# Two-part products one column part at a time, and 512-column products on normalised operands in the dense layers with 512 tokens

## The chip, the cores and the metric

The kernel runs on one core of one Trainium2 chip. The metric is device time in microseconds for one execution; lower is better. A second number, the span, runs from the first to the last instruction of one profiled execution.

## What is computed

The reference is a network of four layers over 512 latent tokens and 256 context tokens, with 1024 channels. Each layer is a token mixer (layers 0 and 3 Fourier, layer 1 differential attention, layer 2 latent attention) followed by a dense layer. Context tokens are updated in layers 0, 1 and 2 by the reference, but layer 3's mixer is the Fourier one, which reads no context in the last layer; so the kernel carries 768 tokens through the dense layers of layers 0 and 1 and 512 through those of layers 2 and 3.

```python
def rms_norm(x, g, eps=RMS_EPS):
    y = x32 * lax.rsqrt(jnp.mean(x32 * x32, axis=-1, keepdims=True) + eps)
    return y.astype(x.dtype) * g
def modulate(x, g, shift, scale):
    return rms_norm(x, g) * (1 + scale) + shift
def sq_relu_mlp(h, w1, w2):
    return jnp.square(jax.nn.relu(h @ w1)) @ w2
...
        x_lat = x_lat + g_m * sq_relu_mlp(modulate(x_lat, norm_mlp_g[i], sh_m, sc_m), mlp_w1[i], mlp_w2[i])
```

`w1` is 1024 x 4096 and `w2` is 4096 x 1024, all in float32.

## The kernel before

Channels lie on the 128 partitions and tokens on the free axis: `x[k]`, k = 0..7, holds 128 channels of all tokens. TensorE multiplies operands of a shortened float32 form, so each operand is split in two tiles, a high part and a low remainder (`split`: ScalarE casts the high part, VectorE subtracts), and every product of 128 rows takes three matmuls: high weight by high operand, high weight by low operand, low weight by high operand. `mm3g` issues them; its loops run over k, then over the three, then over the column parts, because one matmul takes at most 512 columns. Each matmul loads its 128 x 128 weights anew: the page counts as many weight loads (PEld) as matmuls (PE).

The dense layer is `mlp`. `MlpNorm.feed` makes its operand `h[k]` (tiles `hhi`, `hlo`, 776 columns): x times gain and scale, not yet divided by the token's norm, and behind the T tokens two columns with the shift vector. `w1(m)`, m = 0..31, multiplies eight `h[k]` into one PSUM tile `pw` of 1024 columns (three such buffers). With 768 tokens its two parts are 512 and 258 columns, with 512 tokens 256 and 258; 24 such pairs make a tile. VectorE copies the two shift columns to `bt` (L420) and multiplies the rest by the tokens' inverse norm `r_all` (L427); ScalarE adds `bt` in a Relu (L431), squares (L432) and casts `ahi`; VectorE forms `alo`. `w2(j)`, j = 0..7, takes four such tiles and multiplies them into eight output groups; `accum` (L371, VectorE) adds gate times result to `x[n]`. With 768 tokens a group is 12 pairs of 512 and 256 columns, with 512 tokens 12 matmuls of 512. The last, `w2(7)`, has code of its own that goes by chunks of 256 tokens.

The order on TensorE is written by hand, as the program is: w1(0) to w1(3), then for each j w1(4j+4), w2(j), w1(4j+5) to w1(4j+7). The other engines are ordered by the framework's scheduler by priority and dependence; `accum` has a raised one. VectorE also computes the next layer's modulation vectors in the dense layers (units of L264, called from `bg`). Weights come by DMA into ring buffers, five high and low pairs.

`lin_part`, which multiplies the Fourier mixer's result by its weights, has the same loops as `mm3g`, with parts of 512 and 256 columns in layer 0.

Of the kernel before, what the change touches and what calls it, by code (L numbers as in the profile page):

```python
# [19 lines left out]
KT = 8  # L20
# [24 lines left out]
def body(ctx: ExitStack, tc, a, out):  # L45
# [65 lines left out]
    def gload(srcs, n=512):  # L111
        """operands in the space that all phases share, for the start of the next phase among others"""
        w = []
        for src in srcs:
            raw = rawt()
            nc.sync.dma_start(raw[:, :n], src)
            hi, lo = (gp.tile([128, 512], F32R, name="g", tag="g", bufs=4) for _ in range(2))
            split(hi[:, :n], lo[:, :n], raw[:, :n])
            w.append((hi, lo))
        return w  # L120
# [26 lines left out]
    def mm3g(o, n, wfn, afn, parts, off=0):  # L147
        for k in range(n):
            (wh, wl), (ah, al) = wfn(k), afn(k)
            for i, (w, v) in enumerate(((wh, ah), (wh, al), (wl, ah))):  # L150
                for c0, w_ in parts:
                    mm(o[:, c0 - off:c0 - off + w_], w, v[:, c0:c0 + w_],
                       k == 0 and i == 0, k == n - 1 and i == 2)
                    yield cost(w_)
# [5 lines left out]
    def mm3(*args, **kw):  # L160
        run(mm3g(*args, **kw))

    class Fill:
        """Tensor-engine work put between the steps of an attention chain. What a generator gives
        first comes after its loads; the loads of the next one are issued when one starts."""
# [10 lines left out]
        def front(self, name, gens):  # L176
            """Ahead of what is held back."""
            i = [q[0] for q in self.q].index(self.held)
            self.q[i:i] = [[name, g, False] for g in gens]
            self.held = None  # L180
            if i < 2:
                self.prime(i)
# [111 lines left out]
    class MixNorm:  # L294
        """x -> h = x * rstd * g * (1 + scale) + shift, split, by chunks of 256 tokens."""
# [36 lines left out]
    class MlpNorm:  # L332
        """h' = x * g * (1 + scale), split, with the shifts in two columns after the tokens; the
        rstd of a token multiplies what a product with h' gives, the shift's product is added."""
# [39 lines left out]
    def out_gemm_g(K, wfn, afn, T, l, ch, norm=None):  # L374
        """x += gate * (W^T a)"""
        wide = state["psum"]["w"][0] >= T
        for n in range(KT):
            for g in ([parts(T)] if wide else [[q] for q in parts(T)]):
                p = pt_("w")
                o = g[0][0]  # L380
                yield from mm3g(p, K, lambda k: wfn(k, n), afn, g, off=o)
                for c0, w in g:
                    accum(n, c0, w, p[:, c0 - o:c0 - o + w], l, ch)
            if norm:
                norm.feed(n)
# [8 lines left out]
    def mlp(l, nm, nn):  # L394
# [4 lines left out]
        with ExitStack() as es:  # L399
# [10 lines left out]
            hparts, po = ([(0, 512), (512, 258)], 0) if T > SL else ([(0, 256), (256, 258)], 256)  # L410
            nbg = [0.0]

            def w1(m):
                w = wload(wp, a["w1"][l, m]) if m else pre.pop("w1")
                p = pt_("w")
                mm3(p, KT, lambda k: (kview if m else hview)(w, k), lambda k: h[k], hparts, off=-po)
# [4 lines left out]
                r = rp.tile([128, T], F32, name="r", tag="r", bufs=2)  # L421
                hi = ap_.tile([128, T], F32R, name="ahi", tag="a")
                lo = ap_.tile([128, T], F32R, name="alo", tag="a")
# [10 lines left out]
                nbg[0] += 1.6  # L434
                bg(int(nbg[0]))
                nbg[0] -= int(nbg[0])
                return hi, lo

            def w2(j, act):
                w = [wload(wp, a["w2"][l, j * CH + i]) for i in range(CH)]  # L440
                wfn = lambda k, n: kview(w[k], n)
                if j < NJ - 1:
                    run(out_gemm_g(CH, wfn, lambda k: act[k], T, l, G_M))
                    return
# [65 lines left out]
    def lin_part(p, w, Y, k0, k1, T):  # L510
        for k in range(k0, k1):
            (wh, wl), (yh, yl) = (hview if type(w) is list else kview)(w, k), Y[k]
            for i, (u, v) in enumerate(((wh, yh), (wh, yl), (wl, yh))):
                for c0, w_ in parts(T):
                    mm(p[:, c0:c0 + w_], u, v[:, c0:c0 + w_], k == 0 and i == 0, k == KT - 1 and i == 2)

    def fold(sp, p, ny, T, ys):
        """two tiles (d' = 0..127 and 256 - d', 128 first) of the product's real part"""
# [40 lines left out]
    def fourier_first(nm):  # L559
        l, T = 0, TT  # L560
        with ExitStack() as es:
# [66 lines left out]
            def mod_pe(ch, w):  # L628
                """a channel's vectors from weights with the inner dimension on partitions"""
# [136 lines left out]
    def transpose_g(p, dst_h, dst_l, q0, k0, n, tag="t"):  # L766
        """dst[:, kt, q0:q0+128] = transposes of the n blocks of p from k0, split."""
# [8 lines left out]
    def diff(l, h, nm):  # L776
        T = TT
        with ExitStack() as es:
# [85 lines left out]
            def gens(i, hd):  # L864
                """k (or q) of the latent tokens, then of the context."""
# [29 lines left out]
            def S(hd, c0, qi, cqi=None):  # L895
                """Weights of 128 latent queries, and with cqi of 128 context queries."""
# [88 lines left out]
            def last(hd, e):  # L985
                """The end of the latent queries of a head."""
# [457 lines left out]
```

## Time and profile before

| what | value |
|---|---|
| median of three runs | 2974.22 us (2969.59 to 2979.68) |
| span of the profiled execution | 2962.0 us |
| median less span | 12.2 us |
| TensorE matmul (PE) busy | 2843.3 us, 96% |
| VectorE (DVE) busy | 1947.8 us, 66% |
| ScalarE (ACT) busy | 1310.6 us, 44% |

The profiled execution has no time of its own on record beside its span; the 12.2 us between the span and the median of the runs lie outside what the profile shows. Matmuls overlap, so PE's busy time is the time in which at least one is under way; how fast they follow one another is read from the starts of matmuls.

### The profile page before, as it was taken

What the parts mean: (1) busy time and instruction counts of PE and PEld (TensorE: products, weight loads), DVE (VectorE), ACT (ScalarE), POOL (GpSimd) and SP (SyncE); (2) the same over time, 40 slices, a digit from 0 to 9 for tenths busy, and PEclk for the clock granted to TensorE, in tenths of its full rate; (3) what the DMA queues carried; (4) which work ended last, traced back from release to release, by engine and by line L of the source; (5) the groups of instructions that cost most, each with busy time, mean ns of one, the idle gap of its engine ahead of it and who ended that gap; (6) DMA issues with size and microseconds to landing.
All of it is one profiled execution on the core that took longest, in us unless ns stands there. A gap on an engine that the chain in (4) does not pass through costs nothing.

```text
span 2962.0 us, 42506 instructions
## 1 busy us (share of the span) xinstructions
PE 2843.3 (96%) x16875; PEld 2459.3 (83%) x16875; DVE 1947.8 (66%) x3468; ACT 1310.6 (44%) x2405; POOL 157.6 (5%) x167
## 2 busy tenths in 40 slices
PE   8999999999999999799999998899899999999998
PEld 5788888888777777688888887788799998799997
DVE  7986656568677767785445448888776665654454
ACT  4542223235565546533233336777643344543342
POOL 0100000002010000100000002000100001100001
PEclk9999999999999999899999999999999999999999
DMA  8453333331111111053333310000175551232231
GB/s 322 148 178 122 108 106 108 126 102 56 48 35 44 39 35 45 30 176 118 123 107 121 107 50 31 22 22 22 57 235 171 165 170 61 72 116 98 79 107 50
DMA packets 93542, 291.30 MB, mean 98 GB/s; under 512 B 10624, under 2 KB 14880, under 8 KB 92832
## 3 DMA queue, kind: packets, MB, share of 16 engines
q1 hardware_dynamic: 90784, 285.44, 28.8%
q0 software_dynamic: 2560, 3.15, 0.5%
q8 instruction: 133, 2.18, 0.3%
q14 instruction: 65, 0.53, 0.1%
HBM read 283.29 MB, written 2.11 MB: 96 GB/s over the span
## 4 chain that ended last, share of the span: by engine, by line
PE 83%; DVE 10%; ACT 4%; issue 1%; DMA 1%; POOL 1%; POOLq 0%; SPq 0%; ACTq 0%; DVEq 0%
PE pw L140 71%; PE ps L140 5%; PE pu L140 5%; PE pu L770 1%; DVE x L371 1%; DVE ptl L97 1%; ACT e L1251 1%; DVE hlo L330 1%; DVE nu L328 1%; DVE mx L1248 1%; ACT pth L96 1%; PE pn L140 0%; DVE wlo L97 0%; POOL nacc L357 0%; DVE qs L846 0%
## 5 line engine op out<-in xcount | busy, mean ns | idle before, releaser
L96 ACT CAST whi<-raw 128x1024 fp32r<-128x1024 f32 (+1 forms) x322 | 311.8, 984 | 1051.8 <-PE pw L140 1010.0
L371 DVE SCALAR_TENSOR_TENSOR x<-pw,mod,x 128x512 f32<-128x512 f32 (+1 forms) x504 | 302.3, 623 | 331.7 <-PE pw L140 330.5
L140 PE MATMUL pw<-hhi,whi 128*128 128x512 f32 (+1 forms) x2112 | 502.8, 315 | 5.1 <-ACT whi L96 3.5
L140 PE MATMUL pw<-hlo,whi 128*128 128x512 f32 (+1 forms) x2112 | 502.4, 314 | 0.0
L140 PE MATMUL pw<-hhi,wlo 128*128 128x512 f32 (+1 forms) x2112 | 502.4, 314 | 0.0
L140 PE MATMUL pw<-ahi,wlo 128*128 128x512 f32 (+1 forms) x1664 | 500.0, 344 | 0.0
L140 PE MATMUL pw<-ahi,whi 128*128 128x512 f32 (+1 forms) x1664 | 496.5, 342 | 0.0
L140 PE MATMUL pw<-alo,whi 128*128 128x512 f32 (+1 forms) x1664 | 494.9, 341 | 0.0
L97 DVE TENSOR_TENSOR wlo<-raw,whi 128x1024 fp32r<-128x1024 f32 (+1 forms) x322 | 361.6, 1140 | 45.8 <-ACT whi L96 42.0
L140 PEld LDWEIGHTS pw<-hhi,whi 128*128 128x128 f32 x2112 | 334.3, 190 | 32.1 <-ACT whi L96 3.9
L140 PEld LDWEIGHTS pw<-hhi,wlo 128*128 128x128 f32 x2112 | 332.9, 190 | 24.1 <-DVE wlo L97 0.3
L140 PEld LDWEIGHTS pw<-hlo,whi 128*128 128x128 f32 x2112 | 333.2, 191 | 23.7
L140 PEld LDWEIGHTS pw<-ahi,whi 128*128 128x128 f32 x1664 | 284.1, 189 | 40.7
L140 PEld LDWEIGHTS pw<-ahi,wlo 128*128 128x128 f32 x1664 | 282.7, 189 | 36.6
L140 PEld LDWEIGHTS pw<-alo,whi 128*128 128x128 f32 x1664 | 281.1, 188 | 38.0
L264 DVE SCALAR_TENSOR_TENSOR raw<-raw,cb 128x1024 f32<-128x1024 f32 x176 | 215.9, 1227 | 84.8 <-DMA raw<-in_modw 82.8
L97 DVE TENSOR_TENSOR alo<-r,ahi 128x768 fp32r<-128x768 f32 (+2 forms) x134 | 105.8, 792 | 84.1 <-ACT ahi L96 83.9
L431 ACT ACTIVATE r<-r,bt 128x512 f32<-128x512 f32 (+1 forms) x196 | 119.1, 640 | 73.5 <-DVE r L427 73.4
L420 DVE COPY bt<-pw 128x2 f32<-128x2 f32 x128 | 20.1, 157 | 196.4 <-PE pw L140 196.3
L264 DVE SCALAR_TENSOR_TENSOR junk<-raw,cb 128x1024 bf16<-128x1024 f32 x96 | 117.1, 1220 | 46.0 <-DMA raw<-in_modw 43.4
L307 POOL TENSOR_TENSOR nacc<-nacc,nsq 128x256 f32<-128x256 f32 x70 | 53.1, 758 | 1767.1 <-ACT nsq L306 1766.6
L97 DVE TENSOR_TENSOR ptl<-pu,pth 128x384 fp32r<-128x384 f32 (+1 forms) x208 | 107.0, 541 | 53.8 <-ACT pth L96 52.0
(321 smaller groups left out, 4336.4 us busy)
## 6 DMA issues: line engine op xcount, KB each, us to landing
raw<-in_w SPq DMA_DIRECT2D x252, 512.0 KB, 3.6
raw<-in_modw SPq DMA_DIRECT2D x176, 512.0 KB, 3.4
wm<-in_msh SPq DMA_DIRECT2D x32, 256.0 KB, 5.9
raw<-in_fw SPq DMA_DIRECT2D x10, 512.0 KB, 4.7
cb<-scr SPq DMA_DIRECT2D x4, 1024.0 KB, 5.4
raw<-in_dwk SPq DMA_DIRECT2D x16, 256.0 KB, 2.7
raw<-in_dwq SPq DMA_DIRECT2D x16, 256.0 KB, 2.8
raw<-in_dwv SPq DMA_DIRECT2D x16, 256.0 KB, 2.7
```

What stands on the lines that cost most here:

```text
L96: nc.scalar.copy(hi, src)
L97: nc.vector.tensor_sub(lo, src, rd(hi))
L140: r = nc.tensor.matmul(o, lhsT, rhs, start=start, stop=stop)
L264: nc.vector.scalar_tensor_tensor(o, m, 1.0, cb[:, v * 1024:(v + 1) * 1024], op0=ALU.mult, op1=ALU.mult, accum_out=mcol(mod[l, ch], v, k))
L307: nc.gpsimd.tensor_tensor(nacc[:, c0:c0 + w], nacc[:, c0:c0 + w], s, op=ALU.add)
L328: nc.vector.scalar_tensor_tensor(u, xs, am, r, op0=ALU.mult, op1=ALU.mult)
L330: nc.vector.scalar_tensor_tensor(lo, u, sh, rd(hi), op0=ALU.add, op1=ALU.subtract)
L371: nc.vector.scalar_tensor_tensor(xs, src, mcol(mod[l, ch], 0 if c0 < SL else 1, n), xs, op0=ALU.mult, op1=ALU.add)
L431: nc.scalar.activation(r[:, c0:c1], r[:, c0:c1], AF.Relu, bias=bt[:, v:v + 1])
L770: nc.tensor.transpose(t[:, i * 128:(i + 1) * 128], p[:, (k0 + i) * 128:(k0 + i + 1) * 128], ident)
L1248: nc.vector.reduce_max(mx, s[:, :T], axis=AX.X)
L1251: nc.scalar.activation(et, s[:, :T], AF.Exp, bias=mx, scale=MLA_SCALE)
```

## The change

`mm3g` and `lin_part` get the column part as outermost loop, so that all matmuls of the first part come ahead of those of the second. In dense layers with 512 tokens, `normed(k)` replaces `h[k]` in place during `w2(0)` by the fully normalised and shifted operand (it reads `x[k]` before `accum` of the same k writes it), and tiles m >= 5 then run as 24 single matmuls of 512 columns, with a Relu straight from PSUM and neither the copy to `bt` nor the multiplication by `r_all`. `tick` is the old end of `w1` under a name. Comments are removed.

```diff
     def mm3g(o, n, wfn, afn, parts, off=0):
-        for k in range(n):
-            (wh, wl), (ah, al) = wfn(k), afn(k)
-            for i, (w, v) in enumerate(((wh, ah), (wh, al), (wl, ah))):
-                for c0, w_ in parts:
+        for c0, w_ in parts:
+            for k in range(n):
+                (wh, wl), (ah, al) = wfn(k), afn(k)
+                for i, (w, v) in enumerate(((wh, ah), (wh, al), (wl, ah))):
                     mm(o[:, c0 - off:c0 - off + w_], w, v[:, c0:c0 + w_],
                        k == 0 and i == 0, k == n - 1 and i == 2)
                     yield cost(w_)
...
-    def out_gemm_g(K, wfn, afn, T, l, ch, norm=None):
-        """x += gate * (W^T a)"""
+    def out_gemm_g(K, wfn, afn, T, l, ch, norm=None, before=None):
...
         for n in range(KT):
+            if before:
+                before(n)
...
+            wide = T == SL
+            late = CH + 1 if wide else FF
...
+                if m >= late:
+                    mm3(p, KT, lambda k: kview(w, k), lambda k: h[k], [(0, T)])
+                    step = 256 if m == CH * NJ - 1 else T
+                    for o in range(0, T, step):
+                        s = slice(o, o + step)
+                        nc.scalar.activation(r[:, s], p[:, s], AF.Relu)
+                        nc.scalar.activation(r[:, s], r[:, s], AF.Square)
+                        split(hi[:, s], lo[:, s], r[:, s])
+                    tick()
+                    return hi, lo
...
+            def normed(k):
+
+                u = rp.tile([128, T], F32, name="cu", tag="cu", bufs=2)
+                hi, lo = (q[:, 0:T] for q in h[k])
+                sh = mcol(mod[l, SH_M], 0, k)
+                nc.vector.scalar_tensor_tensor(
+                    u, x[k][:, 0:T], mcol(amul[l, SC_M], 0, k), r_all, op0=ALU.mult, op1=ALU.mult)
+                nc.scalar.activation(hi, u, AF.Identity, bias=sh)
+                nc.vector.scalar_tensor_tensor(lo, u, sh, rd(hi), op0=ALU.add, op1=ALU.subtract)
...
-                    run(out_gemm_g(CH, wfn, lambda k: act[k], T, l, G_M))
+                    run(out_gemm_g(CH, wfn, lambda k: act[k], T, l, G_M, before=normed if wide and j == 0 else None))
...
     def lin_part(p, w, Y, k0, k1, T):
-        for k in range(k0, k1):
-            (wh, wl), (yh, yl) = (hview if type(w) is list else kview)(w, k), Y[k]
-            for i, (u, v) in enumerate(((wh, yh), (wh, yl), (wl, yh))):
-                for c0, w_ in parts(T):
+        for c0, w_ in parts(T):
+            for k in range(k0, k1):
+                (wh, wl), (yh, yl) = (hview if type(w) is list else kview)(w, k), Y[k]
+                for i, (u, v) in enumerate(((wh, yh), (wh, yl), (wl, yh))):
                     mm(p[:, c0:c0 + w_], u, v[:, c0:c0 + w_], k == 0 and i == 0, k == KT - 1 and i == 2)
```

On TensorE, at the start of the first output group of w2(0) in layer 0 (names: PSUM tile, then moving operand and weights), the order was, before:

```order
L140 MATMUL pw<-ahi,whi 128x512
L140 MATMUL pw<-ahi,whi 128x256
L140 MATMUL pw<-alo,whi 128x512
L140 MATMUL pw<-alo,whi 128x256
L140 MATMUL pw<-ahi,wlo 128x512
L140 MATMUL pw<-ahi,wlo 128x256
```

In the changed program the same group has twelve of 512 columns and then twelve of 256; the rows at the seam are:

```order
L140 MATMUL pw<-ahi,whi 128x512
L140 MATMUL pw<-alo,whi 128x512
L140 MATMUL pw<-ahi,wlo 128x512
L140 MATMUL pw<-ahi,whi 128x256
L140 MATMUL pw<-alo,whi 128x256
L140 MATMUL pw<-ahi,wlo 128x256
```

The number of matmuls is the same; a matmul now follows one of its own width everywhere but at the seam.

On TensorE in layer 2, where w2(0) ends and w1(5) begins, before:

```order
L140 MATMUL pw<-alo,whi 128x512
L140 MATMUL pw<-ahi,wlo 128x512
L140 MATMUL pw<-hhi,whi 128x256
L140 MATMUL pw<-hhi,whi 128x258
L140 MATMUL pw<-hlo,whi 128x256
L140 MATMUL pw<-hlo,whi 128x258
L140 MATMUL pw<-hhi,wlo 128x256
L140 MATMUL pw<-hhi,wlo 128x258
```

and in the changed program:

```order
L140 MATMUL pw<-alo,whi 128x512
L140 MATMUL pw<-ahi,wlo 128x512
L140 MATMUL pw<-hhi,whi 128x512
L140 MATMUL pw<-hlo,whi 128x512
L140 MATMUL pw<-hhi,wlo 128x512
```

Two matmuls of half the width became one; the operands `hhi` and `hlo` are now those that `normed` writes while w2(0) runs.

On VectorE in layer 2, over w2(0) (x_70 to x_77 are the eight tiles `x[k]`, L371 is `accum`, L264 a unit of the modulation), before:

```order
L371 SCALAR_TENSOR_TENSOR x_70<-pw,mod_5_116,x_70 128x512
L264 SCALAR_TENSOR_TENSOR raw,mod_0_117<-raw,cb 128x1024
L97 TENSOR_TENSOR alo<-r,ahi 128x512
L371 SCALAR_TENSOR_TENSOR x_71<-pw,mod_5_116,x_71 128x512
L264 SCALAR_TENSOR_TENSOR raw,mod_0_117<-raw,cb 128x1024 x2
L371 SCALAR_TENSOR_TENSOR x_72<-pw,mod_5_116,x_72 128x512
L371 SCALAR_TENSOR_TENSOR x_73<-pw,mod_5_116,x_73 128x512
```

and in the changed program, from the last piece ahead of x_74 on:

```order
L371 SCALAR_TENSOR_TENSOR x_74<-pw,mod_5_116,x_74 128x512
L464 SCALAR_TENSOR_TENSOR hlo<-cu,mod_3_113,hhi 128x512
L461 SCALAR_TENSOR_TENSOR cu<-x_77,am_4_115,rall 128x512
L371 SCALAR_TENSOR_TENSOR x_75<-pw,mod_5_116,x_75 128x512
L264 SCALAR_TENSOR_TENSOR raw,mod_0_117<-raw,cb 128x1024
L464 SCALAR_TENSOR_TENSOR hlo<-cu,mod_3_113,hhi 128x512
L371 SCALAR_TENSOR_TENSOR x_76<-pw,mod_5_116,x_76 128x512
```

Two pieces for each k (L461, L464) stand between the additions, those of the last k behind the addition to x_75; most units of the modulation have moved behind them.

## Rows read from the trace of the kernel before

**Rows 1.** The page: busy time, TensorE's granted clock in 40 slices, the chain

```profile
PE 2843.3 (96%) x16875; PEld 2459.3 (83%) x16875; DVE 1947.8 (66%) x3468; ACT 1310.6 (44%) x2405; POOL 157.6 (5%) x167
...
PEclk9999999999999999899999999999999999999999
...
PE 83%; DVE 10%; ACT 4%; issue 1%; DMA 1%; POOL 1%; POOLq 0%; SPq 0%; ACTq 0%; DVEq 0%
```

**Rows 2.** Windows: dense layers 0, 2; length, busy PE PEld DVE ACT POOL, clock, DMA

```profile
177.69:694.87 517.18, 517.18 (x2966) 452.78 (x2965) 330.23 (x516) 161.91 (x212) 5.34 (x8) 1.00 0.35 117
2147.99:2495.30 347.31, 347.31 (x2289) 320.89 (x2290) 220.18 (x334) 130.71 (x176) 5.42 (x8) 0.99 0.50 166
```

**Rows 3.** Timeline of PE, layer 0: first matmuls of w1(5), w2(1), w1(9)

```profile
247.33 0.51 PE L140 MATMUL pw<-hhi,whi 128*128 128x512 f32 x2
...
281.12 0.51 PE L140 MATMUL pw<-ahi,whi 128*128 128x512 f32 x2
...
315.04 0.40 PE L140 MATMUL pw<-hhi,whi 128*128 128x512 f32 x1
```

**Rows 4.** Timeline of PE, layer 2: first matmuls of w1(5), w2(1), w1(9)

```profile
2193.93 0.40 PE L140 MATMUL pw<-hhi,whi 128*128 128x256 f32 x2
...
2216.83 0.40 PE L140 MATMUL pw<-ahi,whi 128*128 128x512 f32 x1
...
2238.62 0.40 PE L140 MATMUL pw<-hhi,whi 128*128 128x256 f32 x2
```

**Rows 5.** Windows: w2(0) of layer 2, w2(0) of layer 3, then layer 3's next four tiles

```profile
2172.14:2193.93 21.79, 21.79 (x99) 18.02 (x97) 15.37 (x24) 5.00 (x7) 0.00 (x0) 1.00 0.61 208
...
2617.03:2638.82 21.79, 21.79 (x99) 18.03 (x97) 8.81 (x12) 5.04 (x7) 0.00 (x0) 1.00 0.07 25
2638.82:2661.78 22.96, 22.96 (x193) 22.96 (x192) 12.34 (x17) 10.90 (x15) 0.00 (x0) 1.00 0.48 161
```

**Rows 6.** Timeline of PE, layer 2's mixer: 512-column run with h, first and last

```profile
1812.52 0.40 PE L140 MATMUL ps<-hlo,whi 128*128 128x512 f32 x1
...
1823.17 0.39 PE L140 MATMUL ps<-hhi,wlo 128*128 128x512 f32 x1
```

**Rows 7.** Timeline of PE, layer 1's mixer: 256-column run with h, first and last

```profile
745.51 0.28 PE L140 MATMUL pw<-hhi,wlo 128*128 128x256 f32 x1
...
749.41 0.28 PE L140 MATMUL pw<-hhi,wlo 128*128 128x256 f32 x1
```

**Rows 8.** Timeline of PE, layer 0's w2(7): 256-column run with activations, first and last

```profile
685.75 0.28 PE L140 MATMUL pw<-ahi,wlo 128*128 128x256 f32 x1
...
691.51 0.28 PE L140 MATMUL pw<-ahi,wlo 128*128 128x256 f32 x1
```

**Rows 9.** Timeline of PE, layer 0's Fourier product by its weights

```profile
95.31 0.52 PE L140 MATMUL pw<-yh,whi 128*128 128x512 f32 x2
...
97.08 0.40 PE L140 MATMUL pw<-yh,wlo 128*128 128x512 f32 x1
```

**Rows 10.** Groups of VectorE and ScalarE by shape: busy us, mean ns, idle before

```profile
L264 DVE SCALAR_TENSOR_TENSOR raw<-raw,cb 128x1024 f32<-128x1024 f32 x176 | 215.9, 1227 | 84.8 <-DMA raw<-in_modw 82.8
L427 DVE TENSOR_TENSOR r<-pw,rall 128x512 f32<-128x512 f32 x62 | 42.1, 681 | 0.0
L348 DVE SCALAR_TENSOR_TENSOR hlo<-x,am,hhi 128x512 fp32r<-128x512 f32 x32 | 23.5, 744 | 2.5 <-ACT hhi L347 2.2
L347 ACT ACTIVATE hhi<-x,am 128x512 fp32r<-128x512 f32 x32 | 23.1, 723 | 43.0 <-DVE x L371 36.1 <-DVE am L254 6.8
```

**Rows 11.** Waits of PE around the start of dense layer 2 (us, times, longest)

```profile
PE pw L140 <- ACT whi L96: 3.5, 1, 3.5
PE pn L140 <- POOL nacc L357: 0.4, 1, 0.4
```

**Rows 12.** Windows: 5.73 us behind PE's wait at the start of dense layer 0

```profile
176.47:182.20 5.73, 5.73 (x17) 4.88 (x18) 5.73 (x13) 2.36 (x4) 0.00 (x0) 0.50 0.73 246
```

More of the change, by code (lines that the diff above doesn't have):

```diff
@@ L409, in mlp, with tick @@
                 bg_add(l + 1, (SC_A, SH_A, G_A, SC_M, SH_M, G_M))
-            hparts, po = ([(0, 512), (512, 258)], 0) if T > SL else ([(0, 256), (256, 258)], 256)
+            wide = T == SL
+            late = CH + 1 if wide else FF
+            hparts, po = ([(0, 256), (256, 258)], 256) if wide else ([(0, 512), (512, 258)], 0)
             nbg = [0.0]
+            def tick():
+                nbg[0] += 1.6
+                bg(int(nbg[0]))
+                nbg[0] -= int(nbg[0])
             def w1(m):
@@ L415, in w1 @@
                 p = pt_("w")
+                r = rp.tile([128, T], F32, name="r", tag="r", bufs=2)
+                hi = ap_.tile([128, T], F32R, name="ahi", tag="a")
+                lo = ap_.tile([128, T], F32R, name="alo", tag="a")
+                if m >= late:
[8 more added lines that the diff above has]
+                    return hi, lo
                 mm3(p, KT, lambda k: (kview if m else hview)(w, k), lambda k: h[k], hparts, off=-po)
@@ L420, in w1 @@
                 nc.vector.tensor_copy(bt, p[:, po + T:po + T + 2])
-                r = rp.tile([128, T], F32, name="r", tag="r", bufs=2)
-                hi = ap_.tile([128, T], F32R, name="ahi", tag="a")
-                lo = ap_.tile([128, T], F32R, name="alo", tag="a")
                 step = 256 if m == CH * NJ - 1 else T
@@ L433, in w1 @@
                     split(hi[:, s], lo[:, s], r[:, s])
-                nbg[0] += 1.6
-                bg(int(nbg[0]))
-                nbg[0] -= int(nbg[0])
+                tick()
                 return hi, lo
+            def normed(k):
[6 more added lines that the diff above has]
+                nc.vector.scalar_tensor_tensor(lo, u, sh, rd(hi), op0=ALU.add, op1=ALU.subtract)
             def w2(j, act):
```

## Prediction

> **What bounds the kernel now.** I read the page first: TensorE is busy 96% of the span, its granted clock is at nine tenths or more in 39 of 40 slices, and the chain that ended last lies on it for 83% [rows 1]. So the time is mostly the number of matmuls times their spacing. Next I cut out the dense layers by windows. In layers 0 and 2, between the start of w1(1) and the end of the whole-group part, PE is busy for the whole length (517.18 of 517.18 us, 347.31 of 347.31) at a clock of 1.00 and 0.99 [rows 2], which is the upper of the two levels, 2.4 GHz. VectorE is busy 64% and 63% of these windows and ScalarE 31% and 38% (330.23 and 161.91 of 517.18, 220.18 and 130.71 of 347.31). There is no gap to fill: here a change is worth what it does to the spacing of matmuls, less any wait that it creates. Third I took the spacing from the timeline, from the first matmul of a block of known size to the first of the next, since PE's busy time counts overlapping matmuls only as "under way".
>
> **The spacings.** A block between two such starts is four tiles of 24 pairs, or eight groups of 12: 96 in each.
> - Layer 0, pairs 512 and 258 (w1): (281.12 - 247.33)/96 = 352.0 ns. Pairs 512 and 256 (w2): (315.04 - 281.12)/96 = 353.3 ns [rows 3].
> - Layers 2 and 3, pairs 256 and 258 (w1): 22.90/96 = 238.5 ns [rows 4] and 22.96/96 = 239.2 ns [rows 5]; mean 238.9.
> - Layer 2, 512 alone with activations (w2): 21.79/96 = 227.0 ns [rows 4].
> - 512 alone with h: from the first to the last row 46 steps in 10.65 us, 231.5 ns [rows 6].
> - 256 alone with h: 33 steps in 3.90 us, 118.2 ns [rows 7]; 258 scaled by columns 119.1.
> - 256 alone with activations: 48 steps in 5.76 us, 120.0 ns [rows 8].
>
> So a pair of different widths costs more than its two halves cost in runs of one width. That is what the sum rests on.
>
> **The change part by part.**
> *A. w2 with 768 tokens.* 2 layers x 7 x 8 groups x 12 = 1344 pairs. Apart, 227.0 + 120.0 = 347.0 ns; together 353.3; so 6.3 ns a pair is to be had. One seam a group stays, so 11 of 12: 1344 x 6.3 x 11/12 = 7.8 us.
> *B. w1 with 768 tokens.* 2 x 32 x 24 = 1536 pairs. Apart, with h, 231.5 + 119.1 = 350.6; together 352.0; 1.4 ns each: 2.2 us. The bounds come from which row the 512 resembles. With h moving, as [rows 6], it is 231.5; at the 227.0 of [rows 4] the gain would be 5.9 ns, 9.1 us. I take the row with the same moving operand.
> *C. w1 with 512 tokens from the sixth tile.* 2 x 27 x 24 = 1296 pairs become single matmuls: 238.9 - 231.5 = 7.4 ns, 9.6 us; 15.4 us if they ran at 227.0.
> *D. The first five tiles there* keep two parts: 2 x 5 x 24 = 240 pairs at 238.9 - (118.2 + 119.1) = 1.6 ns: 0.4 us.
> *E. The Fourier product of layer 0*, 8 x 24 = 192 pairs: five steps in 1.77 us are 354.0 ns [rows 9]. Between nothing and 7.0 ns (the activations' 347.0): 0 to 1.3 us, I take 0.5.
> *F. The first tile of each dense layer.* With the part outermost, w1(0) wants all eight h[k] within its first half, not spread over the tile. In layers 0 and 1 the first part is 24 x 0.23 = 5.5 us of the 8.4. In layer 2 PE waits 3.5 us for weights and 0.4 for the norm at the start [rows 11], so most of a later w1(0) would only shorten the next wait. Below: nothing. Above: 4 us, about the two waits together once more. I take 1.0 us lost. The 5.73 us at a clock of 0.50 (the level of 1.2 GHz) that stand behind PE's wait for the norm in layer 0 [rows 12] are there in both versions, as that wait is for the statistics, not for h.
>
> *What the normalising costs.* `normed` adds, per k, a VectorE piece into `cu`, a ScalarE piece and a second VectorE piece. Nearest rows: 744 ns (L348) and 723 ns (L347) [rows 10]. Eight of each are 8 x 2 x 0.744 = 11.9 us of VectorE and 5.8 us of ScalarE, inside w2(0), which lasts 21.79 us. VectorE has 15.37 us of work there in layer 2 and 8.81 in layer 3 [rows 5]; with 11.9 more, 27.3 and 20.7 us. In layer 3 it fits. In layer 2 it is 5.5 us too much, but the units of the modulation (1.23 us each, L264 [rows 10]) are wanted only by the next layer, and in the changed order most stand behind the normalising. The last piece of k = 7 stands behind the addition to x_75, the sixth group, which ends 6 x 2.72 = 16.3 us into w2(0); three or four VectorE pieces later, about 20 us in, `h[7]` is there. w1(5) begins at 21.8 and needs k = 7 after 21 matmuls, at 26.6. So some 6 us of slack cover it, and I cost it at nothing; without that cover it is the slower rival below. What queues behind these pieces on VectorE is the addition that frees a PSUM buffer of w2(0); with three buffers and 2.72 us a group it may be two groups late, 5.4 us, and one or two pieces of 0.744 delay it by at most 1.5.
>
> *What goes.* 54 tiles lose the multiplication (681 ns [rows 10]) and the small copy on VectorE. That is not on the path. The Relu reads PSUM itself, so the way from the last matmul to `ahi` becomes shorter. DMA issues are unchanged; layer 2 runs 2% faster with DMA engines half busy, so weights keep up.
>
> **Sum.** 7.8 + 2.2 + 9.6 + 0.4 + 0.5 - 1.0 = 19.5 us. Against the profiled span of 2962.0 that gives 2942.5; the median lies 12.2 us above the span, and nothing in the change touches what lies outside it, so 2974.2 - 19.5 = 2954.7 us. Measurement tells about 0.3%, 8.9 us, from no change: faster means below 2965.3.
>
> **The rivals.**
> *Only width counts.* The order of parts is worth nothing, and the differences of A and B come from what each run reads, not from alternation. For: in B the excess is only 1.4 ns, and the rows of single runs come from other stages with other operands. Against: 256 alone is 118 to 120 ns whichever operand moves. Then the 512 within a pair costs what is left: 352.0 - 119.9 = 232.1 in w1, 353.3 - 119.0 = 234.3 in w2 (halves of 238.9 by columns). C alone remains: 1296 x 4.6 to 6.8 ns = 6.0 to 8.8 us, less 1.0: 2966 to 2969, centre 2967. The Trainium skill, "TensorE: Matmul & The Clock Gate", section "Back-to-back issue gap", has such a rule: the gap is the columns at 2.4 GHz plus 2.5 ns, whatever stands beside. By it A and B are worth nothing and C 109.2 + 110.0 - 215.8 = 3.4 ns, 4.4 us, an estimate of 2970 us. This trace's 120.0 and 227.0 ns lie about 11 ns above the page's figures for both widths, and the pair's 6.3 ns excess has no place in the rule, so the measurement decides and I give the rival less than the forecast.
> *All 512 runs reach 227.0 with h too.* For: w2 shows that such a spacing is possible at this clock. Against: [rows 6] show 231.5 with h. C becomes 15.4, B 9.1: 7.8 + 9.1 + 15.4 + 0.4 + 0.5 - 1.0 = 32.2, 2942 us.
> *VectorE or the start takes part of it back.* Layer 2's w2(0) holds the 5.5 us excess on the path instead of shifting it: 2960 us.
> *Slower: the normalising does not overlap w2(0).* If all eight chains began only when w2(0) had ended, w1(5) would wait for 0.744 + 0.723 + 0.744 = 2.2 us eight times, 17.7 us in each of layers 2 and 3, and resume at half clock; a stretch as in [rows 12], 5.73 us at 0.50, costs half of it, 2.9. Twice 20.6 less 19.5 is 21.7: 2996 us. It decides from 9.8 us a layer on. The order speaks against it: the pieces stand among the additions, not behind them.
>
> **How the numbers follow.** Forecast 0.55 (its own range 2949 to 2960); only width 0.22; all at 227.0 0.13; partly taken back 0.07; slower 0.03. The range reaches from just inside the 227.0 case to the width case: 2943 to 2969. Faster by over 0.3%: 0.55 + 0.13 + 0.07 and a fifth of the width case (its lower end), 0.79; the same 0.18; slower 0.03.
>
> **What the profile would show.** Blocks of w2 in layers 0 and 1 of 33.3 us instead of 33.92, of w1 there 33.65 instead of 33.79, and of w1 in layers 2 and 3 22.2 instead of 22.9; w2 there still 21.79. No wait of PE at w1(5) in layers 2 and 3, and L464 for the last k ending before w1(5) begins or shortly after. Clock unchanged. The prediction is wrong if the pair's excess stays with the parts apart (blocks of layers 0 and 1 unchanged), if 512 with h in the dense layers is not near 231.5, or if PE waits on `hhi` or `hlo` behind w2(0).

## The result, and the profile after

The changed kernel took 2955.01 us (median of 4 runs, 2954.13 to 2960.89) against 2974.32 us of before on the same chip: ratio 0.9937, 95% interval 0.992 to 0.9955, so 13 to 24 us less. 2954.7 had been forecast. A second measurement (sixth experiment) gave 2956.05 against 2969.24, ratio 0.9956 (0.994 to 0.9972), 8 to 18 us less. The rows below show that the agreement within 0.3 us is partly chance: stretches that the forecast made about 20 us shorter (its items A to D) became 12.9 and 14.7 us shorter in two traces, and 1.4 us of that only moved elsewhere.

The page of the changed kernel: busy time, granted clock, chain (as [rows 1]).

```profile
PE 2830.2 (96%) x15579; PEld 2396.2 (81%) x15579; DVE 1930.2 (65%) x3390; ACT 1304.7 (44%) x2421; POOL 156.7 (5%) x167
...
PEclk9999999999899999899999999999999999999999
...
PE 82%; DVE 11%; ACT 4%; issue 2%; DMA 1%; POOL 0%; POOLq 0%; SPq 0%; ACTq 0%; DVEq 0%
```

1296 matmuls are gone (16875 to 15579), as many as pairs became single, and PE still bounds the kernel.

The timeline of PE in the changed kernel, the first matmuls of blocks in layer 0 (w2(1), w1(9)) and layer 2 (w1(5), w2(1), w1(9)), to be set beside [rows 3, 4].

```profile
281.81 0.39 PE L140 MATMUL pw<-ahi,whi 128*128 128x512 f32 x1
...
315.26 0.40 PE L140 MATMUL pw<-hhi,whi 128*128 128x512 f32 x1
...
2194.40 0.40 PE L140 MATMUL pw<-hhi,whi 128*128 128x512 f32 x1
...
2216.66 0.40 PE L140 MATMUL pw<-ahi,whi 128*128 128x512 f32 x1
...
2238.47 0.40 PE L140 MATMUL pw<-hhi,whi 128*128 128x512 f32 x1
```

Windows of the changed kernel: w2(1) and w1(9 to 12) of layer 0; then of layer 2 w1(1 to 4), w2(0), w1(5 to 8); of layer 3 w1(5 to 8). The columns are as in [rows 2]: length, then busy time and number of instructions by engine, clock, DMA.

```profile
281.81:315.26 33.45, 33.45 (x195) 29.51 (x193) 17.87 (x30) 4.87 (x7) 0.00 (x0) 1.00 0.20 63
315.26:349.10 33.84, 33.84 (x195) 29.64 (x193) 24.28 (x33) 14.49 (x19) 0.00 (x0) 1.00 0.51 156
...
2145.82:2169.93 24.11, 23.35 (x192) 23.15 (x193) 22.12 (x38) 13.30 (x20) 0.00 (x0) 1.00 0.76 259
...
2169.93:2194.40 24.47, 22.38 (x98) 17.95 (x97) 22.76 (x35) 11.81 (x17) 0.00 (x0) 1.00 0.38 125
2194.40:2216.66 22.26, 22.26 (x97) 18.07 (x96) 15.88 (x21) 11.37 (x16) 0.00 (x0) 1.00 0.77 265
...
2635.67:2657.91 22.24, 22.24 (x98) 18.04 (x97) 10.06 (x11) 10.26 (x15) 0.00 (x0) 1.00 0.51 166
```

w2 of layer 0 went from 33.92 to 33.45 us, w1 of layers 2 and 3 from 22.9 to 22.25. w1 of layer 0 is not shorter but 0.05 longer, and w2(0) of layer 2 has grown from 21.79 to 24.47, of which 2.09 PE stands idle.

**Where the rest of the span moves.** For every trace I added up four windows, each from the start of w1(1) to the last stretch of w2(7) of a dense layer. The number behind "sum" is their length together: the kernel before, the changed kernel, and the changed kernel measured again.

```profile
sum 1753.19, PE 1753.15 PEld 1571.21 DVE 1018.36 ACT 597.98 POOL 32.24; mean PE 438.29 PEld 392.80 DVE 254.59 ACT 149.49 POOL 8.06
```

```profile
sum 1740.25, PE 1736.89 PEld 1504.77 DVE 998.59 ACT 592.40 POOL 32.16; mean PE 434.22 PEld 376.19 DVE 249.65 ACT 148.10 POOL 8.04
```

```profile
sum 1738.54, PE 1736.83 PEld 1504.86 DVE 998.35 ACT 592.69 POOL 32.15; mean PE 434.21 PEld 376.22 DVE 249.59 ACT 148.17 POOL 8.04
```

So 12.9 and 14.7 us in the dense windows. A second trace of before (third experiment) has 1753.50 there. The sums of before thus repeat to 0.3 us, those of the changed kernel to 1.7, mainly in w2(0) of layer 2 (24.47 and 22.55 us); whole runs of one kernel scatter over 3 to 15.

The windows leave out w1(0). In the changed kernel that tile waits three times for `hlo` in layer 2, and the wait for weights behind it has shrunk from 3.5 us [rows 11] to 1.5:

```profile
PE pw L140 <- DVE hlo L348: 2.6, 3, 1.3
PE pw L140 <- ACT whi L96: 1.5, 1, 1.5
```

From the first matmul of w1(0) to that of w1(1) it takes 13.19 us instead of 11.75, and w1(1 to 4) then takes 24.11 instead of 25.42. All five traces with the old order in that tile have 11.70 to 11.88, all nine with the new one 13.17 to 13.20. So 1.4 us of the windows' gain only moved out of them.

The scatter of whole runs lies in the mixers: of the 6.0 us between the spans of the two traces of before, 5.7 lie outside the dense windows. The stretch of layer 1's mixer, between two dense windows, has the same matmuls in every kernel; before, the changed kernel measured again, and the kernel of the fourth experiment:

```profile
707.05:1268.12 561.07, 520.37 (x2775) 412.16 (x2773) 405.48 (x842) 317.02 (x769) 58.77 (x62) 0.94 0.15 43
```

```profile
705.23:1262.39 557.16, 515.66 (x2774) 409.37 (x2773) 405.20 (x842) 316.67 (x769) 59.52 (x62) 0.95 0.15 43
```

```profile
705.29:1274.43 569.14, 528.31 (x2774) 419.80 (x2773) 405.60 (x842) 317.53 (x769) 58.72 (x62) 0.92 0.15 43
```

557 to 569 us. PE stands idle about 41 us in each; what differs is its busy time, and that goes with the granted clock, 0.95 down to 0.92: how much of a mixer runs at the lower level, 1.2 GHz, differs from execution to execution.

### The profile page after: what moved, and what is told of

Same layout as the page of the kernel before. It is cut to its first block, busy times and chain, and to the rows that moved or that the text cites. A ratio compares the mean times of both kernels' runs of the same rounds, so it can differ in the third digit from the quotient of the medians.

```text
span 2953.5 us, 39827 instructions
## 1 busy us (share of the span) xinstructions
PE 2830.2 (96%) x15579; PEld 2396.2 (81%) x15579; DVE 1930.2 (65%) x3390; ACT 1304.7 (44%) x2421; POOL 156.7 (5%) x167
## 4 chain that ended last, share of the span: by engine, by line
PE 82%; DVE 11%; ACT 4%; issue 2%; DMA 1%; POOL 0%; POOLq 0%; SPq 0%; ACTq 0%; DVEq 0%
PE pw L140 70%; PE ps L140 6%; PE pu L140 5%; PE pu L797 2%; DVE x L371 1%; DVE ptl L97 1%; DVE wlo L97 1%; DVE nu L328 1%; DVE hlo L330 1%; ACT e L1278 1%; DVE mx L1275 1%; ACT pth L96 1%; DVE hlo L348 0%; PE pn L140 0%; DVE raw L264 0%
## 5 line engine op out<-in xcount | busy, mean ns | idle before, releaser
L140 PE MATMUL pw<-hhi,whi 128*128 128x512 f32 (+2 forms) x1680 | 590.8, 352 | 3.0 <-ACT whi L96 1.5
L140 PE MATMUL pw<-hlo,whi 128*128 128x512 f32 (+2 forms) x1680 | 589.8, 351 | 0.0
L140 PE MATMUL pw<-hhi,wlo 128*128 128x512 f32 (+2 forms) x1680 | 587.4, 350 | 0.8 <-DVE wlo L97 0.8
L140 PE MATMUL pw<-ahi,whi 128*128 128x512 f32 (+1 forms) x1664 | 568.7, 342 | 1.2 <-ACT ahi L96 1.2
L140 PE MATMUL pw<-alo,whi 128*128 128x512 f32 (+1 forms) x1664 | 567.3, 341 | 1.4 <-DVE alo L97 1.4
L140 PE MATMUL pw<-ahi,wlo 128*128 128x512 f32 (+1 forms) x1664 | 566.2, 340 | 0.0
L371 DVE SCALAR_TENSOR_TENSOR x<-pw,mod,x 128x512 f32<-128x512 f32 (+1 forms) x504 | 302.2, 623 | 291.8 <-PE pw L140 290.7
L140 PEld LDWEIGHTS pw<-alo,whi 128*128 128x128 f32 x1664 | 315.4, 190 | 37.4 <-DVE alo L97 1.9
L140 PEld LDWEIGHTS pw<-ahi,wlo 128*128 128x128 f32 x1664 | 315.0, 189 | 36.2
L264 DVE SCALAR_TENSOR_TENSOR raw<-raw,cb 128x1024 f32<-128x1024 f32 x176 | 216.2, 1228 | 117.3 <-DMA raw<-in_modw 115.4
L264 DVE SCALAR_TENSOR_TENSOR junk<-raw,cb 128x1024 bf16<-128x1024 f32 x96 | 117.2, 1221 | 67.2 <-DMA raw<-in_modw 65.4
L797 PE MATMUL pu<-ident,e 128*128 128x128 f32 x576 | 91.0, 283 | 19.1 <-ACT e L1278 12.1
L96 ACT CAST pth<-pu 128x384 fp32r<-128x384 f32 (+1 forms) x208 | 91.3, 471 | 38.1 <-PE pu L797 36.4
```

What stands on the lines that cost most here:

```text
L96: nc.scalar.copy(hi, src)
L140: r = nc.tensor.matmul(o, lhsT, rhs, start=start, stop=stop)
L264: nc.vector.scalar_tensor_tensor(o, m, 1.0, cb[:, v * 1024:(v + 1) * 1024], op0=ALU.mult, op1=ALU.mult, accum_out=mcol(mod[l, ch], v, k))
L371: nc.vector.scalar_tensor_tensor(xs, src, mcol(mod[l, ch], 0 if c0 < SL else 1, n), xs, op0=ALU.mult, op1=ALU.add)
L797: nc.tensor.transpose(t[:, i * 128:(i + 1) * 128], p[:, (k0 + i) * 128:(k0 + i + 1) * 128], ident)
```

## The experiments

Edits are shown against the changed kernel, or against before where the text says so. Each whole time stands beside one of before on the same chip.

**1. The order of parts alone**, against the changed kernel:

```diff
-            late = CH + 1 if wide else FF
+            late = FF
...
-                    run(out_gemm_g(CH, wfn, lambda k: act[k], T, l, G_M, before=normed if wide and j == 0 else None))
+                    run(out_gemm_g(CH, wfn, lambda k: act[k], T, l, G_M, before=None))
```

> The part-by-part order alone (products and Fourier product), no normalised operands: all dense tiles of layers 2 and 3 keep their pairs of 256 and 258. Theory (a pair of two widths costs more than two runs of one width): 7.8 us in w2 of layers 0 and 1, 2.2 in their w1, 1536 x 1.6 ns = 2.5 in w1 of layers 2 and 3, 0.5 in the Fourier product, less 1.0 at the starts: 12.0 us, 2962 us. Rival (only width counts): 2974 to 2975 us, blocks of w2 in layer 0 still 33.9 us.

Measured: 2972.18 us (12 runs) against 2971.23, ratio 1.0001 (0.9988 to 1.0013): no difference in time, at most 4 us less. But the dense windows sum to 1745.99, 7.2 us less than before (5.8 with w1(0) of layer 2), with w2 blocks at 33.45. The later tiles of layers 2 and 3, pairs of 256 and 258 columns, gained nothing to speak of (blocks of 22.99 and 22.84 us against 22.91 and 22.96). Both the theory's 2962 and the rival's unchanged blocks were wrong. What the blocks gave was lost outside the windows, and scatter alone does not explain it, as the interval leaves no room for 5.8: the clock of the whole execution was 0.975 or lower in 9 of these 12 executions, but in 8 of the 35 of before, and the profiled one's mixer of layer 1 took 568.52 us at 0.92, 7.5 more than in the record of before. Why this kernel met the lower clock more often was not tried.

**2. The 512-column products alone.** The changed kernel with the loops of before in `mm3g` (below) and `lin_part`.

```diff
-        for c0, w_ in parts:
-            for k in range(n):
+        for k in range(n):
...
+                for c0, w_ in parts:
```

> The 512-column products on normalised operands alone, with the old order of the loops everywhere. Theory: 1296 x 7.4 ns = 9.6 us, 2965 us, and together with the order-only kernel the two gains add up to that of the whole change (19.3 us) within the intervals. Rival (only width counts): 6.0 to 8.8 us here, and the order-only kernel at nothing. Rival (the normalising takes part back): a wait of PE in w2(0) or at w1(5) of layer 2 here too, and not in the order-only kernel.

Measured: 2959.08 us, ratio 0.9955 (0.9941 to 0.9968), 9 to 18 us less. Blocks of w1 in layers 2 and 3 take 22.26 and 22.24 us as in the changed kernel, about 9 us in all: theory and size agree. The dense windows, 1743.35, are 9.8 less than before, but 1.3 of this lies in w1(1 to 4) of layer 0, which has the same order in both kernels and took 35.0 to 36.5 us from trace to trace. With experiment 1 the two sum to 17.0. Without that 1.3, and 0.3 in pairs that only experiment 1 still has, it is 15.4, against the change's 12.9 and 14.7: the rest is given back in w2(0) of layer 2 (experiments 6 to 8).

**3. Before again.**

> The kernel before, unchanged, for a second trace of it. The changed kernel's runs lie 2.0 us above their spans, the span of before on record 12.2 us below its median. Theory: the record of before was a short execution of about 2964 us, times of before scatter by 10 us or more, and this trace's span lies 2 us below its own time, somewhere from 2962 to 2978; the difference sits in a few waits or stretches at the lower clock in layer starts and mixers, not in the spacing of dense blocks (33.8 and 33.9 us in layer 0). Rival: before has 12 us outside its span, and its span is 2962 again at a time of 2974.

Measured: 2972.08 us against 2971.23, ratio 1.0005. The profiled execution took 2970.11 us with a span of 2968.0. So 2.1 us lie outside a span, not 12.2 as the text ahead of the prediction has it: the record in [rows 1] was then of a short execution, some 2964 us, below most times of before. The theory held for the offset and for the dense blocks; its mixer of layer 1 was not the longer one, the extra 6 us lay in later stages.

**4. h aligned.** In `MlpNorm`, for 512 tokens, each tile of h is used from a column on that puts its start at the weights' residue of 512 bytes (`q` is the tile's own residue, from the program's addresses):

```diff
+            if T == SL:
...
+                d = [[(96 - q) % 512 // 4 for q in p] for p in at]
+                self.h = [tuple(q[:, e:e + T + 2] for q, e in zip(h, dk)) for h, dk in zip(self.h, d)]
```

> The changed kernel, with the operand h of dense layers 2 and 3 moved by 0 to 127 columns within its tiles, so that every h[k] starts at the same residue of 512 bytes as the weights (the activations do, h has a stride of 3104 bytes and does not). Theory (the 231.5 ns of 512 columns with h against 227.0 with activations comes from where the operand lies): 22 us blocks of w1 there fall to 21.8, 1296 x 4.5 ns = 5.8 us, 2949 us. Rival (it comes from anything else, as the kind of operand or the weights' loading): no change, 2955 us, blocks unchanged at 22.2 to 22.3 us.

Measured: 2950.33 us, ratio 0.993 (0.9913 to 0.9947). The block w1(5 to 8) of layer 2:

```profile
2201.75:2223.51 21.76, 21.76 (x98) 18.02 (x96) 16.21 (x22) 11.46 (x16) 0.00 (x0) 1.00 0.80 271
```

226.7 ns a matmul against 231.9: the theory held, by rows as well as by the dense windows (1732.10 against 1740.25 and 1738.54). **Experiment 12** puts h at one common residue, but another than the weights':

```diff
-                d = [[(96 - q) % 512 // 4 for q in p] for p in at]
+                d = [[(224 - q) % 512 // 4 for q in p] for p in at]
```

> The changed kernel with h of dense layers 2 and 3 moved within its tiles to one common residue of 512 bytes, but another (224) than that of the weights (96). Theory (what counts is that operand and weights lie at the same residue): w1 blocks of 512 columns there at 22.2 us as in the changed kernel. Rival (what counts is that all moving operands lie alike): 21.8 us as in the aligned kernel.

```profile
2193.48:2215.87 22.39, 22.39 (x97) 18.02 (x96) 16.47 (x22) 11.37 (x16) 0.00 (x0) 1.00 0.81 266
```

233.2 ns, slower than with the scattered residues (whole time, a single run, 2955.42 us). What counts is where the moving operand lies with respect to the weights (or something that goes with it in these three programs), not that operands lie alike.

**5. Arrangements.** In layers 0 and 1, `mm3g` gives out `per` matmuls of one part, then `per` of the other, from block to block in another way.

```diff
+        stages = [parts]
+        if len(parts) > 1 and way in (2, 3):
+            stages = [[(0, 256)], [(256, 256), (512, parts[-1][1])]]
+        per = {0: 1, 1: 3 * n, 2: 1, 3: 3 * n, 4: 3, 5: 6}[way]
...
+                                   way=1 if wide else (0, 1, 2, 3, 4, 5, 0)[j]))
```

> The changed kernel; only in dense layers 0 and 1 the order of a product's parts differs from block to block: w2(0) to w2(6), and likewise the four-tile blocks of w1 from w1(5) on, use in turn 0 matmul by matmul (as before the change), 1 part by part (as after), 2 the first 256 columns apart and the other two 256 alternating, 3 three parts of 256 one after another, 4 three of one part then three of the other, 5 six and six, 0 again. Theory (a change of width costs about 2.5 ns, twice a pair): w2 blocks of 33.9, 33.4, 34.6, 34.6, 33.6, 33.5, 33.9 us; with h no order matters, 33.8 in all but ways 2 and 3. Rival (going to and fro between two outputs and two slices of the operand costs, whatever their width): way 2 longer than way 3 by 0.4 to 0.5 us. Rival (nothing to do with the order but with neighbouring waits): blocks do not follow the ways.

Windows of w2(0) to w2(6) of layer 0, ways 0, 1, 2, 3, 4, 5, 0 (in layer 1 the same to 0.05 us; the whole time, a single run, was 2973.80 us):

```profile
215.01:248.93 33.92, 33.92 (x195) 29.43 (x194) 25.82 (x43) 7.19 (x9) 0.00 (x0) 1.00 0.34 111
282.72:316.16 33.44, 33.44 (x194) 29.50 (x193) 17.45 (x30) 4.70 (x7) 0.00 (x0) 1.00 0.19 63
350.00:384.55 34.55, 34.55 (x290) 34.55 (x289) 19.25 (x32) 6.05 (x8) 0.00 (x0) 1.00 0.23 77
418.90:453.45 34.55, 34.55 (x290) 34.55 (x289) 17.97 (x31) 4.82 (x7) 0.00 (x0) 1.00 0.20 68
487.73:521.33 33.60, 33.60 (x194) 29.41 (x193) 21.98 (x38) 6.92 (x8) 0.00 (x0) 1.00 0.24 79
555.06:588.96 33.90, 33.90 (x194) 29.50 (x193) 19.32 (x32) 6.15 (x8) 0.00 (x0) 1.00 0.21 70
622.87:656.16 33.29, 33.29 (x194) 29.10 (x193) 17.35 (x28) 7.12 (x9) 0.00 (x0) 1.00 0.15 48
```

Going to and fro costs nothing at equal width (ways 2 and 3 equal). But the theory of a price per change of width fails twice: way 5, with a sixth of the changes of way 0, takes as long (33.90), and way 0 itself takes 33.92 at the first place and 33.29 at the last, less than part by part. 33.29/96 = 346.8 ns is what the halves cost alone (347.0 in the prediction). Ways 4 and 5 were each entered in one way only, so their 33.60 and 33.90 say little of themselves, as the next two experiments show. Blocks of w1 took 33.79, 33.84, 34.35, 34.27, 33.73 and 33.91 us in ways 0 to 5, near the theory.

**9 and 10. How a block is entered.** Both are the kernel before, w2 alternating matmul by matmul; `per` is as in 5. In 9 only the tile of w1 ahead of each w2(j) has another order, in 10 all tiles of w1 in layers 0 and 1 from the second on go in sixes.

```diff
-                mm3(p, KT, lambda k: (kview if m else hview)(w, k), lambda k: h[k], hparts, off=-po)
+                mm3(p, KT, lambda k: (kview if m else hview)(w, k), lambda k: h[k], hparts, off=-po,
+                    per=(24, 6, 3, 1, 6, 12, 6)[m // 4 - 1] if T > SL and m % 4 == 0 and m else 1)
```

> The kernel before, with w2 alternating matmul by matmul everywhere; in layers 0 and 1 only the tile of w1 just ahead of w2(0) to w2(6) has another order: in turn part by part, six and six, three and three, alternating, six and six, twelve and twelve, six and six. Theory (the spacing of an alternating block depends on how it is entered: the same order took 353.3 ns a pair in the first block of the fifth kernel and 346.7 in its last, entered from six and six): blocks of 33.3 us in w2(1), w2(4) and w2(6), 33.9 in w2(3), the others one or the other. Rival (it depends on the place in the program or on addresses): 33.9 us in all, or a pattern that does not follow the entry. Rival (change of width costs): 33.9 in all.

> The kernel before, with w2 alternating matmul by matmul and all tiles of w1 from the second on in layers 0 and 1 in the order six of 512 columns, six of 258. Theory (entry decides): all 14 blocks of w2 at 346.7 ns a pair, 33.3 us, as the last of the fifth kernel, and blocks of w1 at 353.2 ns, 33.9 us. Rival (place or addresses): w2 at 33.9 us but for single blocks. Rival (change of width costs): 33.9 us throughout.

Experiment 9, w2(0), (1), (2), (3), (5) of layer 0, entered from a tile part by part, in sixes, in threes, alternating, in twelves:

```profile
214.76:248.68 33.92, 33.92 (x195) 29.40 (x193) 25.97 (x43) 7.18 (x9) 0.00 (x0) 1.00 0.33 110
282.50:315.79 33.29, 33.29 (x195) 29.11 (x193) 19.80 (x32) 7.12 (x9) 0.00 (x0) 1.00 0.20 63
349.55:382.84 33.29, 33.29 (x194) 29.10 (x193) 20.37 (x33) 7.13 (x9) 0.00 (x0) 1.00 0.23 79
416.62:450.54 33.92, 33.92 (x195) 29.43 (x193) 20.22 (x33) 7.04 (x9) 0.00 (x0) 1.00 0.21 70
...
551.43:585.35 33.92, 33.92 (x194) 29.40 (x193) 20.27 (x32) 7.18 (x9) 0.00 (x0) 1.00 0.21 71
```

w2(4) and w2(6), entered from sixes, are 33.29 as well, and layer 1 repeats the pattern. In experiment 10 all 14 blocks are short, w2(0) of layer 0 for one:

```profile
212.83:246.12 33.29, 33.29 (x195) 29.11 (x193) 26.19 (x43) 7.13 (x9) 0.00 (x0) 1.00 0.35 111
```

The same 192 matmuls in the same order take 33.92 or 33.29 us by the order of the tile ahead of them. Place in the program is ruled out; the theory held in each of 28 blocks, and the 14 of experiment 11 are 33.29 too. In the short rhythm every pair takes 343 to 350 ns, in the long one every third takes 360 or 361. (Whole times, single runs: 2972.38 and 2959.33 us, before beside them 2963.57; they tell nothing against the mixers' scatter.)

The order ahead is not all there is to it. The Fourier product of layer 0 alternates 512 and 256 columns in before too, and 48 of its pairs, the same in the same program, took 346.9 ns each in the first trace of before and 353.3 in the second:

```profile
128.27:144.92 16.65, 16.65 (x99) 14.67 (x97) 16.65 (x31) 5.57 (x10) 3.68 (x2) 1.00 0.44 148
```

```profile
128.28:145.24 16.96, 16.96 (x98) 14.72 (x97) 16.96 (x31) 5.57 (x10) 4.00 (x2) 1.00 0.45 149
```

So both rhythms stood in the trace that the prediction was made from.

**6, 7, 8. The wait in w2(0) of layer 2.** 6 is the changed kernel, unchanged. 7 is experiment 4 with six landing buffers for weights (`raw`) in layers 2 and 3:

```diff
-            phase(es, f"m{l}", 4, {"w": (1024, 3), "n": (512, 2)}, {"v": 1, "t": 1, "u": 3})
+            phase(es, f"m{l}", 6 if T == SL else 4, {"w": (1024, 3), "n": (512, 2)}, {"v": 1, "t": 1, "u": 3})
```

8 is experiment 4 with `late = 2 * CH + 1` for 512 tokens and `before=normed` at j == 1 in place of j == 0.

> The changed kernel, unchanged, on the same chip as the two below. Theory (its gain is the spacing's 16 us net in the dense layers, and the mixers scatter by about 9 us from execution to execution in both kernels): a median of 2955 to 2960 us with single runs from 2950 to 2963, before at 2971 to 2974. Rival (the first measurement was of lucky runs): median above 2962 us.

> The changed kernel with h aligned as in the fourth kernel and six instead of four landing buffers for the weights in dense layers 2 and 3. Theory (PE's wait for the activations in w2(0) of layer 2, 2.1 us in the changed kernel, is ScalarE standing at casts of weights that have not landed, since a load can only be issued when a buffer is free): that wait goes to nothing and its block from 24.5 to 21.8 us, about 2.5 us better than aligned alone, 2947 us. Rival (the transfers themselves are the limit there, at 259 GB/s): the wait stays, 2950 us.

> The changed kernel with h aligned, and the normalising done during w2(1) instead of w2(0), so that 512-column tiles begin with the tenth. Theory (weights that land late make the wait in w2(0) of layer 2, not the normalising): the wait is still there within 1 us, and 8 tiles x 24 x (239 - 226.5) ns = 2.4 us are lost against aligned alone: 2952.7 us. Rival (the normalising pieces on VectorE and ScalarE make the wait): it is gone, 2.1 to 2.7 us come back, and the time is equal to aligned alone.

Measured: 2956.05, 2953.14 and 2957.00 us, ratios 0.9956 (0.994 to 0.9972), 0.9939 (0.9922 to 0.9956), 0.9959 (0.9942 to 0.9977). The times do not tell the three apart; the waits say more. In the changed kernel PE's waits from w2(0) on, and ScalarE's timeline ahead of them, were:

```profile
PE pw L140 <- ACT ahi L96: 1.2, 1, 1.2
PE pw L140 <- DVE alo L97: 0.8, 1, 0.8
```

```profile
2169.17 1.06 ACT L96 CAST whi<-raw 128x1024 fp32r<-128x1024 f32 x1 [0.51 <-DMA raw<-in_w]
...
2171.82 1.04 ACT L96 CAST whi<-raw 128x1024 fp32r<-128x1024 f32 x1 [1.06 <-DMA raw<-in_w]
2172.77 0.61 ACT L96 CAST ahi<-r 128x512 fp32r<-128x512 f32 x1
```

The cast `ahi` that PE needs stands behind a weight cast that waits for its transfer. In 7 no wait is left; in 8, with the normalising moved, both are there:

```profile
2175.46:2197.25 21.79, 21.79 (x99) 18.02 (x97) 21.38 (x33) 9.86 (x13) 0.00 (x0) 1.00 0.34 120
```

```profile
PE pw L140 <- DVE alo L97: 0.8, 1, 0.8
PE pw L140 <- ACT ahi L96: 0.6, 1, 0.6
```

In this trace, then, the weights were late, and in 8 the wait came without the pieces of `normed`, so they are not its only cause. That six buffers cure it is likely but not shown, because the wait differs from trace to trace. With six it was nothing in both traces (7 and 11, w2(0) of 21.79 us). With four it was 2.0 and 0.4 us in the two traces of the changed kernel, 1.4 in 8, 0.8 in 4, 0.3 in 5, 0.2 in 2, and nothing in 1 and 12 (21.84 and 22.01 us). In time 7 is not told apart from 4: its dense windows sum to 1731.83 against 1732.10, as w1(1 to 4) of layer 3 took 0.6 us longer with six buffers (23.86 us in 7 and 11, 23.30 in 4); why was not tried.

**11. What the runs point to, together**: 7, with w2 of layers 0 and 1 alternating and entered by a tile in threes, the other tiles of w1 alternating (`per=0` is part by part).

```diff
-                mm3(p, KT, lambda k: (kview if m else hview)(w, k), lambda k: h[k], hparts, off=-po)
+                mm3(p, KT, lambda k: (kview if m else hview)(w, k), lambda k: h[k], hparts, off=-po,
+                    per=0 if wide or not m else 3 if m % 4 == 0 else 1)
...
-                yield from mm3g(p, K, lambda k: wfn(k, n), afn, g, off=o)
+                yield from mm3g(p, K, lambda k: wfn(k, n), afn, g, off=o, per=1)
```

> The changed kernel with what the runs point to: h aligned and six landing buffers in dense layers 2 and 3 as in the seventh kernel, and in layers 0 and 1 w2 alternating matmul by matmul, entered by a tile of w1 in threes (three of 512, three of 258), the other tiles of w1 alternating. Theory: blocks of w2 there at 33.3 us instead of 33.4 (14 x 0.15 = 2.1 us), of w1 at 33.8 (1 us), so the four dense windows together take 1729 us against 1732 of the aligned kernel, 1739 of the changed one and 1753 of before; the median near 2947 us, with the mixers' scatter of 8 us on top of each run. Rival (entry does not carry over in the changed kernel): w2 blocks at 33.9, dense windows 1738 us.

Measured: 2951.91 us (2942.66 to 2955.83) against 2972.54, ratio 0.9928 (0.9913 to 0.9943). Dense windows:

```profile
sum 1726.02, PE 1724.97 PEld 1497.68 DVE 1000.71 ACT 598.63 POOL 32.15; mean PE 431.24 PEld 374.42 DVE 250.18 ACT 149.66 POOL 8.04
```

That is 27.2 us under before and 12.5 to 14.2 under the changed kernel. It is 5.8 us under 7, where 3.1 had been expected; 2.5 of the difference lie in w1(1 to 4) and w2(7) of layer 0, which differ from trace to trace, so the excess is not shown to be the edit's. It beats before clearly, by 17 to 26 us in time. Against the changed kernel the intervals of the times overlap, and only the dense windows show a difference.

## Why the prediction was right, and where it was not

- **A, w2 with 768 tokens: 7.8 us forecast, 14 blocks x 0.47 = 6.6 measured.** Size near, cause wrong. The step "a pair of different widths costs more than its two halves cost in runs of one width" fell: the alternating order costs 346.8 ns a pair, no more than the halves, when entered from threes or sixes, and 353.3 when entered from alternating, twelves or part by part (9, 10). Before was in the slow rhythm in all 14 blocks. Part by part took 348.4, entered from alternating (5) or from part by part: in runs of twelve, 512 columns cost 229.0 and not 227.0, and 256 cost 119.3 (medians of the 112 groups). The trace of before had spoken against the step: the 48 pairs at 346.9 lie behind the six of [rows 9] in the same product. That A gained at all is the luck of the rhythm that before was in: against the other, part by part would have lost 1.6 ns a pair.
- **B, w1 with 768 tokens: 2.2 forecast, -0.8 measured** (352.5 ns a pair against 352.0, 1536 pairs). The halves came from mixers, 231.5 and 118.2 scaled to 119.1. In w1(9) of layer 0 in the changed kernel the runs of 512 and of 258 begin at 315.26 and 320.82, the next tile at 323.72: 231.7 ns a matmul, as forecast, and 120.8, so the scaled term was mis-sized. No order tried brought these tiles below 351.
- **C, 512 columns from the sixth tile: 9.6 forecast, 1296 x (238.9 - 231.9) = 9.1 measured.** Right, and whole times show it too (experiment 2). The rival of 227.0 was open for a reason the prediction did not have: it needs the operand elsewhere in its tile (4, 12).
- **D and E: 0.9 forecast.** w1(1 to 4) of layer 3 went from 23.15 to 23.03. E gave next to nothing: the last 150 of the 192 pairs took 52.38 and 52.70 us in the two traces of before, 52.30 in both of the changed kernel. Six pairs at 354.0 had stood for all.
- **F, the first tile: 1.0 lost forecast.** Its mechanism held: in layer 2 w1(0) became 1.4 us longer and the stretch behind it 1.3 shorter, 0.1 lost together. In layers 0 and 1 the lengths of w1(0) scatter by over 1 us in kernels of either order.
- **Costed at nothing: the normalising.** It hid, as forecast. No wait at w1(5), and the last `hlo` (L464), below with its duration and first and last start, began at 2191.5 and so ended 22.3 us after w2(0) had begun (about 20 forecast), some 7 us ahead of the matmul that needs it, the 22nd after 2194.40:

```profile
L464 DVE SCALAR_TENSOR_TENSOR hlo<-cu,mod,hhi x8: 739/742/746, 2175.3 to 2191.5; 128x512 fp32r<-128x512 f32 x8
```

- **Missed: w2(0) of layer 2 and w2(7) of layer 0.** PE met the weights' transfers: w2(0) lost 2.7 us, in the second trace 0.8 (22.55). I had costed it by VectorE alone and not by ScalarE's queue. w2(7) of layer 0 lost 0.8 (16.19 to 17.02), 0.5 of it a wait for `alo`; the cause is open.
- **Sum.** 6.6 - 0.8 + 9.1 + 0.1 + 1.3 - 2.7 - 0.8 = 12.8, the 12.9 of the dense windows; the 1.3 is the start of layer 2 and is paid back in w1(0). The forecast for the same stretches was about 20, of its sum of 19.5. The whole time fell by 19.3 us in one measurement and by 13.2 in the other, and the first agrees with the forecast by luck, as the windows hold only 12.9 to 14.7 of it. "The median lies 12.2 us above the span" was taken as fixed, but 10 of the 12.2 were the scatter of executions (3).
- **The rival "only width counts"** gave nothing for A and was wrong there, by rows; its doubt about alternation was right in substance. The Trainium skill, "TensorE: Matmul & The Clock Gate", section "Back-to-back issue gap", cited at that rival, has gaps that go by the number of columns alone, and calls the formula used there the isolated gap. This case has 346.8 and 353.3 ns for one pair, and 226.7 to 233.2 ns for 512 columns, so here the measurement decides.

What stays open: what sets the rhythm and carries it from one block to the next, what in the addresses makes 226.7 ns into 231.9 or 233.2, and why the order-only kernel met the lower clock more often.

## What to carry to other kernels

Where an engine is busy to the last microsecond, measure the spacing of its instructions block by block and over every block of a kind, and test a supposed cause by the same order in another place before building on it: here one order had two spacings. Before a row stands for a class, look for other rows of the same instructions in the same trace. Compare changes of half a per cent in windows that repeat (0.3 to 1.7 us here) as well as in whole times that scatter by ten, and look at what lies just outside a window: a gain inside can be a wait that moved, and a kernel can gain 7 us in its windows and nothing in its time. Where a stage gets faster at its start, look at what is loaded there, on the queue of the engine that converts it.

## What the runs showed of the hardware

- 192 alternating matmuls of 512 and 256 columns in the same order take 33.29 or 33.92 us, by the order of the 48 ahead of them (42 blocks, no exception). Both spacings also come without any difference in order: 48 pairs of one program took 16.65 us in one execution and 16.96 in another.
- 512 columns of these operands take 226.7 ns a matmul when operand and weights start at the same residue of 512 bytes (96), 233.2 when h lies at 224, and 231.9 on average when its tiles lie at 16 different ones.
- The same mixer took 557 to 569 us at granted clocks of 0.95 to 0.92.
